# Splitting 20 of the 24 weights of k, r and v during the first FFN, with a round trip through DRAM

## The chip, the cores and the metric

The kernel runs on one core of a Trainium2 chip. TensorE (PE) does the matmuls, VectorE (DVE) and ScalarE (ACT) the elementwise work, GpSimd (POOL) small preparations and some transfers; SyncE (SP) only issues transfers. The metric is the device time of one execution in microseconds, the median of several runs.

## The reference

A trunk of two layers over 512 tokens of width 1024, in fp32: a gated linear recurrence (RG-LRU), a gated conv-FFN, an RWKV-7 time mixing, a second conv-FFN, and a norm. The change concerns the FFN and the first products of RWKV-7:

```
def _conv_ffn(x, norm, w_up, conv_w, conv_b, w_down):
    h = _rmsnorm(x, norm)
    u = jnp.einsum('btd,df->btf', h, w_up)
    gate = _causal_dwconv(u[..., :D_FF], conv_w, conv_b)
    hid = jax.nn.gelu(gate, approximate=True) * u[..., D_FF:]
    return jnp.einsum('btf,fd->btd', hid, w_down)

def _rwkv7_block(...):
    xs_rkv = jnp.stack([h + xx * mix[0], h + xx * mix[1], h + xx * mix[2]])
    rkv = jnp.einsum('sbtd,sde->sbte', xs_rkv, w_rkv)
    ...
    y = _rwkv7_scan(rh, hs(decay), kh, vh, -kk, kk * ah)
    ...
    return jnp.einsum('btd,de->bte', y * g, w_out)
```

## The kernel before

**Products.** A product of fp32 matrices is made of three matmuls of rounded parts (mm3, matmuls at L54): a weight's high part with the activation's high and low part, and its low part with the high part. So every weight must be split: ACT casts the raw piece to its high part (wh, L94) and DVE subtracts that from the raw piece (wl, L97). A piece is 512 KB, 128 partitions x 1024 numbers, and so are wh and wl.

**Weights.** plan_weights (L100) lists all pieces in the order of use. Numbers 33 to 100 are the first FFN's, 101 to 108 those of k, 109 to 116 of r, 117 to 124 of v, 125 to 132 of RWKV's output, and then the second FFN's. weights_load (L160) issues the raw piece's load on SP's queue (L166); a few FFN pieces have a second part that POOL adds to them in a transfer (L168). weights_split (L172) does the two splitting instructions. Each product calls next_weights, which loads up to three pieces ahead and splits two ahead. raw, wh and wl (and hi, lo of the FFN's Halves pairs) all live in one ring of 21 slots, b4: a load waits until the last reader of its slot's former content is done, which is a DVE subtraction for a raw piece and a matmul for a split one.

**Stages by time of the profile.** RG-LRU until about 163 us; the first FFN until 548; RWKV-7 until 893 (k until about 613, r until 687, v until 745, then the chunks of the scan and the output); the second FFN to the end. In the FFN, 12 pairs of column blocks are made; every second pair from the third on (Halves, L676 to L785) shares products to save matmuls, and after each of those follows down(n), the product with w_down, which runs between the products of the next pair. Such a round takes 63.75 us. In down, a call between runs the next pair's products up to its third, and a call then makes the weights of what follows.

**Order.** The order of instructions on each engine is the program's, made when the kernel is built: tasks in lanes are pushed (L59) and advanced by background (L62), a few steps after each product. In RWKV the lanes hold the preparation of k and r for the scan, and solve (L1258), a chain of DVE and PE steps for each half of the heads: solve(0) while r is made, solve(1) while v is made. In RWKV the engine POOL makes selectors (sel, selk), masks (L1367), the start of the solve's X (L1297) and copies (tu, rts).

Of the kernel before, what the change touches and what calls it, by code (L numbers as in the profile page):

```python
# [7 lines left out]
F32 = mybir.dt.float32  # L8
F32R = mybir.dt.float32r
# [4 lines left out]
DRAM = bass.MemoryType.DRAM  # L14
NOSYNC = mybir.DependencyInfo(mybir.DependencyClass.NoSync, mybir.DependencyReason.DATA)

P = 128
D = 1024
# [10 lines left out]
WARM2 = 20  # L29
WARM = 14  # L30

HALVES = (3, 5, 7, 9, 11)
# [12 lines left out]
class Kernel:  # L45
# [54 lines left out]
    def plan_weights(self):  # L100
# [45 lines left out]
        full(I["lru_w_out"][0], [0, 1])  # L146
        ffn(0)
        for i in (1, 0):
            full(I["rwkv_w_rkv"][0, i], [0, 1])
# [7 lines left out]
        self.plan = plan  # L157
        self.loaded, self.splitted = {}, {}
        self.n_load = self.n_split = self.n_used = 0

    def weights_load(self, upto):
        while self.n_load < min(upto, len(self.plan)):
            i = self.n_load
            src, k, _, more = self.plan[i]
            raw = self.b4(F32, (k, D // k), f"raw{i}")
            self.nc.sync.dma_start(raw, src)  # L166
            if more is not None:
                self.nc.gpsimd.dma_start(raw, more, accum_op=ALU.add)  # L168
            self.loaded[i] = raw
            self.n_load += 1  # L170

    def weights_split(self, upto, pin=False):  # L172
        while self.n_split < min(upto, len(self.plan)):
            i = self.n_split
            if self.plan[i][2]:
                self.n_split += 1
                continue
            self.weights_load(i + 1)
            raw = self.loaded.pop(i)
            k = self.plan[i][1]  # L180
            hi = self.b4(F32R, (k, D // k), f"wh{i}")
            lo = self.b4(F32R, (k, D // k), f"wl{i}")
            for j in range(k) if i == 0 else [slice(0, k)]:
                self.split(raw[:, j], hi[:, j], lo[:, j], pin=pin)
            self.splitted[i] = (hi, lo)
            self.n_split += 1
# [46 lines left out]
    def setup(self):  # L233
# [4 lines left out]
        self.xsp = ctx.enter_context(tc.tile_pool(name="xsp", bufs=1))  # L238
        dram = ctx.enter_context(tc.tile_pool(name="dram", bufs=1, space=DRAM))
        self.xd = dram.tile([P, KB, T], F32, name="xd")  # L240
# [345 lines left out]
    def ffn(self, l, xs, finish, after=None):  # L586
        nc, tc = self.nc, self.tc
        last = l == 1
        with tc.tile_pool(name=f"ffn{l}", bufs=1) as pool:
# [3 lines left out]
            rbs, norm = [], []  # L593
            gpads = [pool.tile([P, 2, T + 2], F32, name=f"gpad{i}") for i in range(2)]
            for u in gpads:
# [80 lines left out]
            class Pair:  # L676

                def __init__(pair, n):
                    pair.n, pair.gp = n, gpads[n % 2]
                    pair.w, pair.bank, pair.s = {}, {}, {}  # L680

                def gate(pair, e):
                    if not e:
                        pair.ge = pool.tile([P, 2, T], F32, tag="ge", name="ge", bufs=2)
                    fb = 2 * pair.n + e
# [11 lines left out]
            class Whole(Pair):  # L697
# [5 lines left out]
                def product(pair, p):  # L703
                    hi, lo = self.next_weights()
                    k0 = int(p[1]) * 4
                    for e in range(2):
# [9 lines left out]
                        if p == "U1":  # L716
# [6 lines left out]
                            self.split(un, pair.hid[:, e, 0], pair.hid[:, e, 1])  # L723
                        self.background(1)

            class Halves(Pair):
# [95 lines left out]
            def down(n, b0, blocks, between, then):  # L822
# [3 lines left out]
                for g in range(2):  # L826
# [28 lines left out]
                    else:  # L855
# [12 lines left out]

                        self.project(hids, ev, kb=blocks, join=2 if g else 1, rate=0.5 if final else 2, after=hook, x0=b0)

            rooms = []

            def room(b):
                if b % 2 == 0:
                    rooms.append(pool.tile([P, 2, 2, T], F32R, tag="xt", name="hx", bufs=4))
                return rooms[-1][:, b % 2, 0], rooms[-1][:, b % 2, 1]

            for n in range(3, 12, 2):
                products((n, 7))
                if n == 11 and not last:  # L880
                    self.norm_begin()
                    self.push(self.lora_weights())
                down(n, 2 * n - 6, 4 if n < 11 else 8, lambda: products((n, 3)), lambda: ahead(at[0] + 2))
            if not last:
# [896 lines left out]
```

## Time and profile before

| what | us |
|---|---|
| runs | 1292.97, 1290.55, 1290.84 |
| median | 1290.84 |
| the profiled execution | 1291.05 |
| its span, first to last instruction | 1289.3 |

The profile is of one execution. Its page has the busy time of each engine, the span in 40 slices, and groups of instructions by line; the trace behind it answers questions for a window, a tile or an engine. A row of a window gives its length, the busy time of each engine with the number of instructions, PE's granted clock (1.00 is full speed), the mean busy share of the core's 16 DMA engines and the GB/s that they moved. In a row of the timeline stand start and duration, engine, line, operation, out<-in and, in brackets, the idle time ahead of it and what ended it. A DMA's time to landing runs from its issue until its data are there.

### The profile page before, as it was taken

To read this page: it belongs to the slowest core of one execution; us is meant where nothing else is said; L and a number is where in the kernel's file an instruction comes from. 1 tells how busy PE (TensorE), PEld (TensorE's weight loads), DVE (VectorE), ACT (ScalarE), POOL (GpSimd) and SP (SyncE) were. 2 spreads that over 40 slices of the span, in tenths; PEclk is the share of its full clock that TensorE was granted. 3 is DMA by queue.
4 is the path that set the end of the run, shared out by engine and by line. 5 is a ranking of instruction groups with operands and counts; after the bars stand their busy time and mean duration, and the time that the engine had idled before them with its cause. 6 is when DMAs were issued, how large, how long until landed. Compare 5 with 4: busy or idle time off the path is not lost. (4 is left out here: it accounts for less than half of the span.)

```text
span 1289.3 us, 22401 instructions
## 1 busy us (share of the span) xinstructions
PE 1264.2 (98%) x9259; PEld 1067.0 (83%) x9259; DVE 928.1 (72%) x1412; ACT 642.8 (50%) x1006; POOL 133.6 (10%) x206
## 2 busy tenths in 40 slices
PE   9999999999999999999899999999999999999998
PEld 8777888989898888877678888778889898988886
DVE  5998678757575766788999967778766566666653
ACT  6797455434343443559844346545644334343432
POOL 3000001010101010010002145410010101010100
PEclk9999999999999999999999999999999999999999
DMA  7312335455454544422212122132344454545431
GB/s 222 111 55 94 98 122 108 150 112 159 103 164 98 170 95 116 144 79 82 79 41 87 52 62 84 44 99 82 116 96 161 101 170 92 178 84 179 100 131 65
DMA packets 117829, 141.37 MB, mean 110 GB/s; under 512 B 10138, under 2 KB 91748, under 8 KB 117600
## 3 DMA queue, kind: packets, MB, share of 16 engines
q1 hardware_dynamic: 100528, 122.44, 29.8%
q0 software_dynamic: 16624, 16.47, 8.4%
q8 instruction: 72, 1.18, 0.4%
q10 hardware_dynamic: 576, 1.05, 0.2%
q14 instruction: 29, 0.24, 0.1%
HBM read 135.41 MB, written 4.52 MB: 109 GB/s over the span
## 5 line engine op out<-in xcount | busy, mean ns | idle before, releaser
L97 DVE TENSOR_TENSOR wl<-raw,wh 128x1024 fp32r<-128x1024 f32 (+1 forms) x161 | 194.4, 1213 | 124.7 <-ACT wh L94 104.0
L94 ACT CAST wh<-raw 128x1024 fp32r<-128x1024 f32 (+1 forms) x161 | 165.9, 1043 | 195.2 <-PE acc L54 56.0
L54 PE MATMUL accG<-xs,wh 128*128 128x512 f32 x448 | 138.7, 391 | 0.0
L54 PE MATMUL accU<-xs,wh 128*128 128x512 f32 x448 | 138.6, 391 | 0.0
L54 PE MATMUL acc<-hid,wh 128*128 128x512 f32 x384 | 119.8, 395 | 0.0
L744 DVE TENSOR_TENSOR lo<-raw,hi 128x1024 fp32r<-128x1024 f32 x70 | 85.5, 1222 | 39.4 <-PE accU L54 32.0
L743 ACT CAST hi<-raw 128x1024 fp32r<-128x1024 f32 x70 | 73.6, 1052 | 60.7 <-PE accU L54 25.3
L54 PEld LDWEIGHTS accG<-xs,wh 128*128 128x128 f32 x448 | 83.7, 188 | 17.3
L54 PEld LDWEIGHTS accU<-xs,wh 128*128 128x128 f32 x448 | 83.7, 188 | 17.2
L54 PE MATMUL accG<-xs,wl 128*128 128x512 f32 x224 | 87.3, 390 | 0.0
L54 PE MATMUL accU<-xs,wl 128*128 128x512 f32 x224 | 87.3, 390 | 0.0
L54 PEld LDWEIGHTS acc<-hid,wh 128*128 128x128 f32 x384 | 71.3, 187 | 16.7
L54 PE MATMUL accA<-xt,hi 128*128 128x256 f32 x480 | 83.4, 277 | 0.0
L54 PE MATMUL acc<-xs,wh 128*128 128x512 f32 x256 | 81.1, 398 | 0.0
L690 DVE SCALAR_TENSOR_TENSOR cv<-gpad,pv,cv 128x512 f32<-128x512 f32 x96 | 69.1, 748 | 12.3 <-ACT cv L688 11.8
L845 PE MATMUL acc<-wl,hid 128*128 128x512 f32 (+1 forms) x200 | 77.2, 386 | 0.0
L844 PE MATMUL acc<-wh,hid 128*128 128x512 f32 (+1 forms) x200 | 77.0, 385 | 0.0
L843 PE MATMUL acc<-wh,hid 128*128 128x512 f32 (+1 forms) x200 | 76.7, 383 | 0.0
L168 POOL DMA_DIRECT2D raw<-in_ffn_w_up_dram x20 | 25.7, 1285 | 480.8 <-DMA raw<-in_ffn_w_up_dram 336.3
L54 PE MATMUL acc<-hid,wl 128*128 128x512 f32 x192 | 75.0, 395 | 0.0
L54 PEld LDWEIGHTS accA<-xt,hi 128*128 128x128 f32 x480 | 73.2, 188 | 0.9
L54 PE MATMUL accA<-xt,lo 128*128 128x256 f32 x240 | 66.3, 276 | 0.0
(411 smaller groups left out, 2943.1 us busy)
## 6 DMA issues: line engine op xcount, KB each, us to landing
raw<-in_ffn_w_up_dram SPq DMA_DIRECT2D x106, 512.0 KB, 3.7
raw<-in_ffn_w_down_dram SPq DMA_DIRECT2D x48, 512.0 KB, 3.9
raw<-in_ffn_w_up_dram POOLq DMA_DIRECT2D x30, 512.0 KB, 5.9
raw<-in_rwkv_w_rkv_dram SPq DMA_DIRECT2D x24, 512.0 KB, 3.7
raw<-in_lru_w_in_dram SPq DMA_DIRECT2D x16, 512.0 KB, 4.3
raw<-in_lru_w_out_dram SPq DMA_DIRECT2D x8, 512.0 KB, 3.7
raw<-in_rwkv_w_out_dram SPq DMA_DIRECT2D x8, 512.0 KB, 3.6
xd<-x SPq DMA_DIRECT2D x8, 256.0 KB, 2.0
```

Source lines behind the costliest of these rows:

```text
L54: mm = lambda *a, **kw: self.nc.tensor.matmul(ps, *a, skip_group_check=more, **kw)
L94: put = (self.nc.vector.tensor_copy if dve else self.nc.scalar.copy)(hi, src)
L97: self.nc.vector.tensor_tensor(lo, src, hi.bitcast(F32), ALU.subtract)
L168: self.nc.gpsimd.dma_start(raw, more, accum_op=ALU.add)
L690: nc.vector.scalar_tensor_tensor(cv, pair.gp[:, e, j : j + T], cw(j), cv, ALU.mult, ALU.add)
L743: nc.scalar.copy(hi, f[p])
L744: tt(lo, f[p], hi.bitcast(F32), ALU.subtract)
L843: nc.tensor.matmul(ps, hh[:, s], wh[:, k, m], start=kk == 0, stop=False)
L844: nc.tensor.matmul(ps, hl[:, s], wh[:, k, m], start=False, stop=False)
L845: nc.tensor.matmul(ps, hh[:, s], wl[:, k, m], start=False, stop=kk == blocks - 1)
```

## The change

A new task, split_ahead, runs in lane 1 from the first FFN's third pair on. For each of the weights 101 to 120 POOL fetches the raw piece into a tile of the FFN's own pool (early, two buffers), ACT and DVE split it into two slots of the ring (eh, el), and POOL stores both parts to DRAM (whd, wld). It advances by 0.19 step per step of down and 0.25 per product of a Whole pair; what is left is drained ahead of the last down. When RWKV comes to such a weight, weights_load has POOL fetch the two parts from DRAM (two transfers of 512 KB) where SP fetched the raw piece before, and weights_split does nothing for it. Room for early is made by one gate pad (gpad) and one ge buffer in the first FFN where there were two. between and then now also split the weights that down needs next, which moves those requests in both FFNs.

```diff
+AHEAD = 20
@@ plan_weights
         ffn(0)
+        self.ahead = range(len(plan), len(plan) + AHEAD)
@@ weights_load
             src, k, _, more = self.plan[i]
+            if i in self.stored:
+                self.loaded[i] = tuple(self.b4(F32R, (k, D // k), f"{part}{i}") for part in ("wh", "wl"))
+                for t, d in zip(self.loaded[i], self.stored[i]):
+                    self.nc.gpsimd.dma_start(t, d)
+                self.n_load += 1
+                continue
             raw = self.b4(F32, (k, D // k), f"raw{i}")
             self.nc.sync.dma_start(raw, src)
...
+    def split_ahead(self, pool):
+
+        raws, parts = {}, {}
+        n = self.ahead.stop
+
+        for i in range(self.ahead.start, n + 2):
+            if i < n:
+                src, k = self.plan[i][:2]
+                raws[i] = pool.tile([P, k, D // k], F32, tag="early", name="early", bufs=2)
+                self.nc.gpsimd.dma_start(raws[i], src)
+            if i - 2 in parts:
+                k = self.plan[i - 2][1]
+                self.stored[i - 2] = [self.dram.tile([P, k, D // k], F32, name=f"{part}d{i - 2}") for part in ("wh", "wl")]
+                for t, d in zip(parts.pop(i - 2), self.stored[i - 2]):
+                    self.nc.gpsimd.dma_start(d, t.bitcast(F32))
+            if i - 1 in raws:
+                k = self.plan[i - 1][1]
+                parts[i - 1] = [self.b4(F32R, (k, D // k), f"{part}{i - 1}") for part in ("eh", "el")]
+                self.split(raws.pop(i - 1), *parts[i - 1])
+            yield 1
@@ weights_split
+            if i in self.stored:
+                self.splitted[i] = raw
+                self.n_split += 1
+                continue
@@ ffn
-            gpads = [pool.tile([P, 2, T + 2], F32, name=f"gpad{i}") for i in range(2)]
+            gpads = [pool.tile([P, 2, T + 2], F32, name=f"gpad{i}") for i in range(1 + l)]
@@ Pair
-                    pair.n, pair.gp = n, gpads[n % 2]
+                    pair.n, pair.gp = n, gpads[n % len(gpads)]
...
-                        pair.ge = pool.tile([P, 2, T], F32, tag="ge", name="ge", bufs=2)
+                        pair.ge = pool.tile([P, 2, T], F32, tag="ge", name="ge", bufs=1 + l)
@@ Whole
                         self.background(1)
+                        self.background(0.25, 1)
@@ down
-                        self.project(hids, ev, kb=blocks, join=2 if g else 1, rate=0.5 if final else 2, after=hook, x0=b0)
+                        self.project(hids, ev, kb=blocks, join=2 if g else 1, rate=0.5 if final else 2, rate1=0 if final else 0.19, after=hook, x0=b0)
@@ the loop over the pairs
+            def between():
+                products((n, 3))
+                if n < 11:
+                    self.weights_split(self.n_used + 2)
+
+            def then():
+
+                if len(seq) > at[0]:
+                    self.weights_split(self.n_used + 2)
+                ahead(at[0] + 2)
+
             for n in range(3, 12, 2):
                 products((n, 7))
+                if n == 3 and not last:
+                    self.push(self.split_ahead(pool), 1)
                 if n == 11 and not last:
+                    while self.tasks[1]:
+                        self.background(1, 1)
                     self.norm_begin()
                     self.push(self.lora_weights())
-                down(n, 2 * n - 6, 4 if n < 11 else 8, lambda: products((n, 3)), lambda: ahead(at[0] + 2))
+                down(n, 2 * n - 6, 4 if n < 11 else 8, between, then)
```

Three places of the order. The first is ACT in the first FFN, in the round whose first down weight is 67. Before, with hi1 to hi7 the casts of the Halves pair, cv and ge its gate, and raw62 to raw66 its pieces:

```order
L743 CAST hi5_3034<-raw63_2951 128x1024
L743 CAST hi6_3074<-raw62_2949 128x1024
L688 ACTIVATE cv_3011<-gpad0_1477,pv_78 128x512
L743 CAST hi2_3106<-raw64_2954 128x1024
L691 ACTIVATE ge_3010<-cv_3011 128x512
L688 ACTIVATE cv_3029<-gpad0_1477,pv_78 128x512
L691 ACTIVATE ge_3010<-cv_3029 128x512
L94 CAST hid_3050<-s_3051 128x512
L743 CAST hi7_3137<-raw65_2956 128x1024
```

And of the change, where the helper's line is L96, Halves' L778 and the gate's L722 and L725:

```order
L96 CAST eh108_3061<-early_2971 128x1024
L778 CAST hi1_3065<-raw62_3015 128x1024
L96 CAST wh61_3069<-raw61_3013 128x1024
L778 CAST hi5_3110<-raw63_3017 128x1024
L96 CAST eh109_3155<-early_3055 128x1024
L722 ACTIVATE cv_3087<-gpad0_1477,pv_78 128x512
L778 CAST hi6_3160<-raw62_3015 128x1024
L722 ACTIVATE cv_3105<-gpad0_1477,pv_78 128x512
L725 ACTIVATE ge_3086<-cv_3087 128x512
L778 CAST hi2_3192<-raw64_3020 128x1024
```

eh108 and eh109 have come in among the casts of the pair, and hi6, hi2 and hi7 now stand behind eh109. In both orders hi4, hi3 and then wh67, the cast of the down weight, follow some rows below.

The second is POOL in the same round. Before it issued only three transfers in a round, each of which adds a second part to a raw piece (raw63, raw65 and raw62 in this one, behind two of the round before):

```order
L168 DMA raw52_2428<-in_ffn_w_up_dram 128x4x256
L748 DMA raw49_2421<-in_ffn_w_up_dram 128x4x256
L168 DMA raw63_2951<-in_ffn_w_up_dram 128x4x256
L168 DMA raw65_2956<-in_ffn_w_up_dram 128x4x256
L748 DMA raw62_2949<-in_ffn_w_up_dram 128x4x256
```

Now the same three stand among stores and fetches:

```order
L177 DMA raw63_3017<-in_ffn_w_up_dram 128x4x256
L195 DMA whd108_3151<-eh108_3061 128x1024
L177 DMA raw65_3022<-in_ffn_w_up_dram 128x4x256
L190 DMA early_3149<-in_rwkv_w_rkv_dram 128x2x512
L195 DMA wld108_3152<-el108_3062 128x1024
L195 DMA whd109_3442<-eh109_3155 128x1024
L190 DMA early_3440<-in_rwkv_w_rkv_dram 128x2x512
L195 DMA wld109_3443<-el109_3156 128x1024
L783 DMA raw62_3015<-in_ffn_w_up_dram 128x4x256
```

So each transfer that adds waits behind what those stores and fetches wait for.

The third is RWKV. ACT before, at the weights 107 and 108 (pinv, fac, sq, ppad and AR belong to the preparation of k and r, mt to the mixing of the input, back to k's norm):

```order
L962 ACTIVATE mt_5389<-x_68,om_451 128x512
L1172 ACTIVATE ppad1_5255<-AR0_4902 128x8x64
L94 CAST wh107_5334<-raw107_5262 128x1024
L1171 ACTIVATE fac_5358<-BK0_4904,oka_452,pv_78 128x512
L1170 ACTIVATE sq_5356<-BK0_4904,pv_78 128x512
L1149 CAST back_5375<-back_5370 40x512
```

ACT now, at the same place:

```order
L1012 ACTIVATE mt_5575<-x_68,om_451 128x512
L1222 ACTIVATE ppad1_5445<-AR0_5100 128x8x64
L1221 ACTIVATE fac_5544<-BK0_5102,oka_452,pv_78 128x512
L1233 COPY AR0_5100<-ppad1_5445 128x4x2x64
L1220 ACTIVATE sq_5542<-BK0_5102,pv_78 128x512
L1199 CAST back_5561<-back_5556 40x512
```

The casts are gone from it. On POOL the fetches stand in their place; at the weights 116 and 117 it now reads:

```order
L171 DMA wl116_6043<-wld116_4130 128x1024
L1417 MEMSET masks_6221 128x384
L1488 COPY rts_6214<-AR0_5100 64x128
L1424 AFFINE_SELECT masks_6221<-masks_6221 64x64 x9
L1488 COPY rts_6214<-AR0_5100 64x128 x3
L171 DMA wh117_6118<-whd117_4213 128x1024
L171 DMA wl117_6119<-wld117_4214 128x1024
```

Before, the masks and copies stood alone there; the loads of the raw pieces were on SP.

More of the change, by code (lines that the diff above doesn't have):

```diff
@@ L157, in plan_weights @@
         self.plan = plan
-        self.loaded, self.splitted = {}, {}
+        self.loaded, self.splitted, self.stored = {}, {}, {}
         self.n_load = self.n_split = self.n_used = 0
@@ L238, in setup @@
         self.xsp = ctx.enter_context(tc.tile_pool(name="xsp", bufs=1))
-        dram = ctx.enter_context(tc.tile_pool(name="dram", bufs=1, space=DRAM))
+        dram = self.dram = ctx.enter_context(tc.tile_pool(name="dram", bufs=1, space=DRAM))
         self.xd = dram.tile([P, KB, T], F32, name="xd")
```

## The prediction

> **What bounds the kernel now.** I read the busy times first, then the slices, then windows by stage, and last the waits of the stage that the change touches.
>
> ```profile
> PE 1264.2 (98%) x9259; PEld 1067.0 (83%) x9259; DVE 928.1 (72%) x1412; ACT 642.8 (50%) x1006; POOL 133.6 (10%) x206
> DVE  5998678757575766788999967778766566666653
> ```
>
> PE is busy 98% of the span; what is left to win is its 2% of idle time and whatever stretches its matmuls. DVE has its row of nines in slices 20 to 23, about 612 to 741 us: the RWKV layer's k, r and v. The windows of that layer and of one 63.75-us round of the first FFN say the same:
>
> ```profile
> 288.75:352.50 63.75, 63.75 (x362) 55.57 (x362) 41.65 (x52) 24.99 (x31) 3.81 (x3) 1.00 0.51 133
> ...
> 613.90:632.00 18.10, 15.04 (x65) 10.88 (x64) 17.05 (x30) 15.19 (x29) 0.00 (x0) 0.91 0.20 65
> 632.00:650.00 18.00, 16.88 (x184) 12.45 (x185) 14.61 (x23) 14.04 (x32) 2.76 (x2) 1.00 0.26 83
> 650.00:677.00 27.00, 25.98 (x119) 19.41 (x118) 26.75 (x59) 11.21 (x17) 1.83 (x6) 1.00 0.15 45
> 677.00:703.40 26.40, 26.40 (x298) 23.32 (x299) 25.79 (x55) 12.33 (x29) 3.39 (x11) 1.00 0.30 96
> 703.40:710.20 6.80, 5.57 (x155) 5.18 (x154) 4.94 (x4) 4.18 (x9) 6.20 (x6) 1.00 0.19 64
> 710.20:744.40 34.20, 30.91 (x606) 27.63 (x604) 32.11 (x78) 13.18 (x25) 3.63 (x9) 1.00 0.14 44
> ```
>
> The columns are length, then busy time of PE, weight loads, DVE, ACT and POOL, then granted clock, DMA share and GB/s. In the FFN, PE is full, DVE has 22.1 us free in a round, ACT 38.8, the DMA engines half. In the six RWKV windows, 130.5 us together, PE is busy 120.78 and DVE 121.25: there DVE is the fuller engine.
>
> Where PE waits there, and for whom:
>
> ```profile
> PE acc L54 <- ACT wh L94: 3.5, 2, 3.0
> PE pe L1462 <- DVE tu L1507: 1.8, 2, 1.1
> PE tr L1432 <- DVE W L1425: 1.5, 1, 1.5
> PE knb L1211 <- DVE rec L1205: 1.2, 1, 1.2
> ```
>
> ```profile
> 615.89 1.03 ACT L94 CAST wh<-raw 128x1024 fp32r<-128x1024 f32 x1
> ...
> 616.97 3.25 PE L54 MATMUL acc<-mix,wh 128*128 128x512 f32 x7 [3.02 <-ACT wh L94]
> ```
>
> ```profile
> 614.00:617.00 3.00, 0.03 (x1) 0.03 (x1) 3.00 (x6) 3.00 (x7) 0.00 (x0) 1.00 0.53 175
> 617.00:621.00 4.00, 4.00 (x11) 3.09 (x11) 4.00 (x7) 4.00 (x9) 0.00 (x0) 0.57 0.03 6
> ```
>
> The longest wait is for the cast of weight 107: ACT, busy all of 614 to 617, comes to it late. PE then runs four microseconds at a granted clock of 0.57.
>
> **The change, part by part.** A split is one cast and one subtraction:
>
> ```profile
> L97 DVE TENSOR_TENSOR wl<-raw,wh 128x1024 fp32r<-128x1024 f32 (+1 forms) x161 | 194.4, 1213 | 124.7 <-ACT wh L94 104.0
> L94 ACT CAST wh<-raw 128x1024 fp32r<-128x1024 f32 (+1 forms) x161 | 165.9, 1043 | 195.2 <-PE acc L54 56.0
> ```
>
> *Taken out of the RWKV layer.* Twenty splits: 20 x 1.21 = 24.3 us of DVE and 20 x 1.04 = 20.9 us of ACT. The subtractions by window:
>
> ```profile
> 613.90:632.00 18.10, 6.51 (x17) 3.15 (x16) 3.65 (x3) 0.91 0.20 65
> 632.00:650.00 18.00, 6.80 (x17) 3.19 (x17) 2.45 (x2) 1.00 0.26 83
> 650.00:677.00 27.00, 13.00 (x34) 6.20 (x33) 4.86 (x4) 1.00 0.15 45
> 677.00:703.40 26.40, 14.48 (x48) 9.09 (x48) 4.88 (x4) 1.00 0.30 96
> 703.40:710.20 6.80, 2.25 (x9) 1.51 (x9) 1.18 (x1) 1.00 0.19 64
> 710.20:744.40 34.20, 11.53 (x41) 7.65 (x41) 2.43 (x2) 1.00 0.14 44
> ```
>
> (The third figure with a count is DVE's on wl.) Between 613.9 and 710.2 the sum is 17.0 us. The two after 710.2 are weights 121 and 122, which are still split there. So:
> - The wait for weight 107 goes, 3.02 us, and with it the low clock, 4 x (1 - 0.57) = 1.7 us. Together 4.7. What is late next there is not a weight (108 comes ready made too) but the key's norm, with 1.2 us of waiting for rec, which DVE feeds.
> - PE's other idle time in the six windows is 9.72 - 3.02 = 6.70 us, and the waits named for it are on DVE results. From below it gives nothing (DVE runs a chain whose links must follow each other); from above all 6.7. The last window keeps its two splits and its 94% of DVE, so I leave its 3.29 us where they are and take the rest, 3.4.
>
> Gain 8.1 us, by these rows between 3 (4.7 less about as much waiting for rec again) and 11.4 (9.72 + 1.7). Matmuls that now run spread out could close up as well; that cannot be more than the 17.0 us that DVE loses.
>
> *Added to the first FFN.* The same 24.3 and 20.9 us, five splits in a round: DVE goes from 41.65 to 47.7 of 63.75 us, ACT from 24.99 to 30.2. Their idle time hides it at no cost; without this cover the price would be the 24.3 us themselves. One gate pad and one ge instead of two cost nothing:
>
> ```profile
> 311.94 2.74 DVE L690 SCALAR_TENSOR_TENSOR cv<-gpad,pv,cv 128x512 f32<-128x512 f32 x4
> ...
> 316.39 1.29 DVE L783 TENSOR_TENSOR s<-s,ge 128x512 f32<-128x512 f32 x2
> ...
> 343.49 0.69 DVE L714 TENSOR_TENSOR gpad<-accG,rb 128x512 f32<-128x512 f32 x1 [0.32 <-PE accG L54]
> ```
>
> The pad's last reader ends at 314.7 and the next pair writes at 343.5; ge is last read until 317.7, and the next pair's is made after that pad. Some 28 us lie between.
>
> *The first down weight of a round* is the tight place, and the order shows that its neighbours move:
>
> ```profile
> 357.14 3.09 SPq L166 DMA_DIRECT2D raw<-in_ffn_w_down_dram  x2
> ...
> 361.91 1.23 DVE L97 TENSOR_TENSOR wl<-raw,wh 128x1024 fp32r<-128x1024 f32 x1 [3.58 <-ACT wh L94]
> ...
> 365.38 0.62 PE L54 MATMUL acc<-hid,wh 128*128 128x512 f32 x2
> ```
>
> Weight 67 is loaded from 357.14 (into the slot that the last piece hi4, lo4 of the pair frees), is split at 363.14 and used at 365.38: 2.24 us to spare, as at 301.68 a round earlier. Now eh109 and el109 stand ahead of that piece on ACT and DVE (1.04 and 1.21 us, part of it in idle time), so I expect some 1.2 us of the margin to go, and 1.0 to remain. Transfers that meet others are slower, by how much the page shows:
>
> ```profile
> raw<-in_ffn_w_up_dram SPq DMA_DIRECT2D x106, 512.0 KB, 3.7
> raw<-in_ffn_w_down_dram SPq DMA_DIRECT2D x48, 512.0 KB, 3.9
> raw<-in_ffn_w_up_dram POOLq DMA_DIRECT2D x30, 512.0 KB, 5.9
> raw<-in_lru_w_in_dram SPq DMA_DIRECT2D x16, 512.0 KB, 4.3
> q1 hardware_dynamic: 100528, 122.44, 29.8%
> q0 software_dynamic: 16624, 16.47, 8.4%
> ```
>
> The first layer's loads, which meet all that the kernel fetches at its start, took 4.3 instead of 3.7: 0.6, within the 1.0. I take 0.5 us for the FFN over all its rounds; from below 0, from above the slower rival's price.
>
> *Transfers.* Five fetches, ten stores of 512 KB in a round are new, all issued by POOL. By the hardware queue's rate (122.44 MB in 29.8% of 1289.3 us: 319 GB/s) one takes 1.64 us of the 16 engines, 15 of them 24.7 us, and the share goes from 0.51 to 0.90. By the software queue's (16.47 MB in 8.4%: 152 GB/s, nearly all transfers that add to what they find) 3.45 us each, share 1.32, more than there is. Plain copies are nearer to the first row. The Trainium skill, "DMA: Bandwidth & Descriptors", Issuing engines are not separate DMA queues, speaks against the change: DMAs of all issuers interleave on the same 16 engines, so POOL's queue keeps nothing out of SP's way. The same page's Anatomy of one DMA — SWDGE (gpsimd) path gives 2.0 us + bytes / 436e3, an estimate of 3.2 us for each of these; the 5.9 us on POOL's queue above disagrees (those add), and by the page the next item's price would be nothing and the sum 0.5 us better.
>
> *Fetches in the RWKV layer* take the place of SP's 20 loads: 40 on POOL, in ring order, each held until its slot is free; selectors, masks, and the solve's X stand behind them in that queue. The one without room is weight 117:
>
> ```profile
> 678.92 1.05 POOL L1438 COPY rts<-AR 64x128 f32<-64x128 f32 x3
> ...
> 687.19 0.28 PE L1250 MATMUL acc<-wh,mix 128*128 128x256 f32 x1
> ```
>
> It stands behind these copies and can go out at about 680.0; with two issues and 5.9 us it lands between 686 and 687.2, and PE wants it at 687.19. Between nothing and some 1.5 us; I take 0.5. Weight 118 is used seven microseconds later and has room.
>
> *The second FFN* keeps its two pads; its down weights are only requested a few rows later. Cost 0.
>
> **The sum**: -4.7 - 3.4 + 0.5 + 0.5 = -7.1 us on the profiled run's own 1291.05 (span 1289.3 and 1.75 around it), 1283.95. The median of the three runs shown is 0.2 lower, 1290.84; I write 1284.
>
> **Rivals.**
> - *Full gain*: DVE is what holds r and v, and without 17 us of splits both solves start sooner. For it: 26.75 of 27.00 and 25.79 of 26.40 us of DVE. Against it: PE is also full in 677 to 703.4. It gives 11.4 us of idle time and clock, and up to 17 with matmuls that close up: 1274 to 1280, near 1278.
> - *Given back*: the wait at 614 moves to rec and to fetches on POOL that are held by their slots; only 0 to 2 us stay, 1289 to 1291. For it: the chain of the second solve fills the last window (32.11 of 34.20) and keeps its splits.
> - *Slower*: the DMA engines become the bound of the FFN. With 49% of 63.75 us free, 31.2 us, fifteen transfers fit if each takes less than 2.08 us of all engines. At 2.4 us, between the two rates, a round misses 4.8 us and four rounds 19; less the 8 gained, 1302. PE would wait for the first down weight of each round. For it: 152 GB/s on that queue. Against it: stores and fetches add nothing to memory.
> - *It does nothing*, because the fetches go out too late: the order has them some weights ahead of their use, except 117, so I give this little.
>
> **How the numbers follow.** Forecast (1280 to 1288) 0.44; full gain 0.16; given back or without effect 0.21; slower 0.19. A measurement tells about 0.2%, 2.6 us, from no change: faster means below 1288.3. Faster gets the first two and a little of the third's lower edge, 0.62; same 0.19; slower 0.19. The range takes in the forecast, the given-back case, most of the full gain and the mild part of the slower one: 1276 to 1297.
>
> **What would show it.** In the changed profile PE's 3.02-us wait near 614 and the low clock behind it are gone; DVE has about 17 us less between 613.9 and 710 and 6 more in each of four FFN rounds; PE stays at 63.75 of 63.75 there; weight 117 is waited for by a microsecond at most. I am wrong if PE waits for wh or wl at the first down weight of a round, if raw pieces on SP take over 4.9 us to land there, or if the stretch from 621 to 744 is as long as before.

## The result, and the profile after

The changed kernel takes 1322.15 us (median of 6 runs, 1321.17 to 1323.92) against 1291.88 of before on the same chip: a ratio of 1.0235, 95% interval 1.0221 to 1.0249. It is 30 us slower, outside the range and on the other side. The profiled run has a span of 1321.5 us, 32.2 more than before. First the page of the changed kernel, busy times, the DMA slices and the queues:

```profile
PE 1281.2 (97%) x9259; PEld 1076.5 (81%) x9259; DVE 929.1 (70%) x1411; ACT 640.1 (48%) x1006; POOL 190.5 (14%) x306
...
DMA  7322444496968678445545120322344546354541
...
q1 hardware_dynamic: 94064, 111.95, 26.6%
q0 software_dynamic: 31024, 68.90, 20.3%
```

DVE and ACT do as much as before. The software queue now has 68.90 MB. If the transfers that it had before still take their 108 us of 16 engines, the 52.43 MB that came on took 20.3% of 1321.5 us less those 108, which is 160 us: an estimate of 328 GB/s, or 1.60 us for 512 KB.

Where the time went is read from the first matmul of one and the same weight in both timelines (before first, then after: weight 101, which opens k, and the first weight of the second FFN):

```profile
572.22 0.62 PE L54 MATMUL acc<-mix,wh 128*128 128x512 f32 x2
...
893.51 0.62 PE L54 MATMUL accG<-xs,wh 128*128 128x512 f32 x2
```

```profile
610.88 0.63 PE L56 MATMUL acc<-mix,wh 128*128 128x512 f32 x2
...
925.10 0.63 PE L56 MATMUL accG<-xs,wh 128*128 128x512 f32 x2
```

At weight 101 the changed kernel is 38.7 us late, at the second FFN 31.6, at the end 32.2. So the stretch up to weight 101, in short the first FFN, lost 38.7 us, RWKV won 7.1, the second FFN cost 0.6. The windows of the changed kernel, the first FFN from where the new task runs, then k, r and v (PE, weight loads, DVE, ACT, POOL, clock, DMA share, GB/s):

```profile
248.00:548.00 300.00, 279.13 (x1485) 237.20 (x1484) 194.20 (x236) 121.30 (x146) 50.82 (x70) 0.97 0.73 217
...
611.00:655.00 44.00, 44.00 (x197) 34.18 (x195) 38.58 (x85) 37.20 (x64) 13.19 (x50) 1.00 0.52 162
655.00:718.00 63.00, 63.00 (x399) 47.86 (x392) 54.74 (x114) 27.38 (x59) 15.58 (x32) 1.00 0.43 140
718.00:776.00 58.00, 56.23 (x1061) 51.39 (x1061) 49.30 (x110) 24.28 (x55) 16.14 (x23) 1.00 0.27 88
```

PE, which had no idle time in the FFN, now misses 20.9 of 300 us there, and the mean clock of 0.97 over the other 279 is some 8 us more. On the whole page PE's busy time grew by 17.0 us (1264.2 before) for the same 9259 matmuls; what stretches them beyond the clock is not shown. In k and r PE is busy all the time. The waits of PE between 225 and 600 us, after:

```profile
PE accU L56 <- ACT wh L96: 11.5, 4, 4.6
PE accA L56 <- ACT s L800: 5.1, 5, 2.6
PE acc L56 <- ACT wh L96: 2.5, 4, 1.0
PE acc L56 <- DVE wl L99: 1.6, 3, 0.5
```

Before, PE waited for no weight of the FFN in this stretch. The largest wait comes once in each of four rounds, at the up weights 48, 61, 74 and 87, one weight ahead of the Halves pair; the first down weight of the round comes after it. One such place, the one with the shortest of the four waits, in the changed kernel's timelines of POOL, ACT and PE:

```profile
275.37 1.32 POOL L177 DMA_DIRECT2D raw<-in_ffn_w_up_dram  x1 [12.32 <-DMA raw<-in_ffn_w_up_dram]
276.16 1.09 POOL L195 DMA_DIRECT2D whd<-eh  x1
```

```profile
282.78 1.04 ACT L96 CAST wh<-raw 128x1024 fp32r<-128x1024 f32 x1 [8.39 <-DMA whd<-eh]
```

```profile
283.88 0.73 PE L56 MATMUL accU<-xs,wh 128*128 128x512 f32 x2 [0.98 <-ACT wh L96]
```

Read backwards: PE waits for wh48; ACT could not cast it, since its ring slot still held an early weight until the store whd had landed; that store went out at 276.16, behind an adding transfer on POOL that had waited 12.32 us for the FFN's own raw piece; and that piece took long to land. In three of the four rounds ACT waits so for a store before it casts this weight, 8.3 to 8.7 us each time. SP's loads wait for the same stores (the longest of SP's waits in the changed kernel, 225 to 560 us):

```profile
SPq L175 <- DMA whd<-eh: 52.2, 4, 13.8
```

And they take longer to land (KB each and median us, between 250 and 540 us; before, then after):

```profile
raw<-in_ffn_w_up_dram SPq DMA_DIRECT2D x32, 512.0 KB, 3.7
```

```profile
raw<-in_ffn_w_up_dram SPq DMA_DIRECT2D x34, 512.0 KB, 9.0
...
wld<-el POOLq DMA_DIRECT2D x20, 512.0 KB, 7.0
```

Three things can thus make the loss: slots of the ring that early weights hold (A), the bytes (B), and the order on the queues, above all POOL's (C). The work of the splits themselves is a fourth (D).

### The profile page after: what moved, and what is told of

It is laid out like the page before. It is cut to its first block, busy times and chain, and to the rows that moved or that the text cites. A ratio compares the mean times of both kernels' runs of the same rounds, so it can differ in the third digit from the quotient of the medians.

```text
span 1321.5 us, 22606 instructions
## 1 busy us (share of the span) xinstructions
PE 1281.2 (97%) x9259; PEld 1076.5 (81%) x9259; DVE 929.1 (70%) x1411; ACT 640.1 (48%) x1006; POOL 190.5 (14%) x306
## 3 DMA queue, kind: packets, MB, share of 16 engines
q0 software_dynamic: 31024, 68.90, 20.3%
## 4 chain that ended last, share of the span: by engine, by line
PE 75%; DVE 9%; DMA 7%; issue 5%; ACT 3%; POOL 1%; SPq 0%; POOLq 0%; DVEq 0%; ACTq 0%
PE acc L56 25%; PE accG L56 9%; PE accU L56 8%; PE accA L56 6%; DMA raw<-in_ffn_w_up_dram 4%; PE acc L880 3%; PE acc L879 3%; PE acc L878 3%; PE accF L56 3%; PE accD L56 1%; DVE wl L99 1%; PE s L1468 1%; DMA whd<-eh 1%; DVE lo L779 1%; PE lg L56 1%
## 5 line engine op out<-in xcount | busy, mean ns | idle before, releaser
L96 ACT CAST wh<-raw 128x1024 fp32r<-128x1024 f32 (+1 forms) x141 | 145.2, 1041 | 178.2 <-DMA raw<-in_ffn_w_down_dram 40.0
L99 DVE TENSOR_TENSOR wl<-raw,wh 128x1024 fp32r<-128x1024 f32 (+1 forms) x141 | 170.0, 1212 | 79.2 <-ACT wh L96 70.6
L56 PE MATMUL accU<-xs,wh 128*128 128x512 f32 x448 | 144.4, 404 | 11.5 <-ACT wh L96 11.5
L56 PEld LDWEIGHTS accU<-xs,wh 128*128 128x128 f32 x448 | 86.7, 195 | 31.0 <-ACT wh L96 13.2
L56 PEld LDWEIGHTS accG<-xs,wh 128*128 128x128 f32 x448 | 83.7, 188 | 17.3
L778 ACT CAST hi<-raw 128x1024 fp32r<-128x1024 f32 x70 | 73.3, 1049 | 42.9 <-PE accU L56 16.1
L56 PE MATMUL accA<-xt,hi 128*128 128x256 f32 x480 | 86.8, 282 | 5.1 <-ACT s L800 5.1
L56 PE MATMUL accU<-xs,wl 128*128 128x512 f32 x224 | 90.3, 403 | 1.1 <-DVE wl L99 1.1
L722 ACT ACTIVATE cv<-gpad,pv 128x512 f32<-128x512 f32 x48 | 38.0, 811 | 66.2 <-DVE gpad L809 40.4
```

The source lines that it names most:

```text
L56: mm = lambda *a, **kw: self.nc.tensor.matmul(ps, *a, skip_group_check=more, **kw)
L96: put = (self.nc.vector.tensor_copy if dve else self.nc.scalar.copy)(hi, src)
L99: self.nc.vector.tensor_tensor(lo, src, hi.bitcast(F32), ALU.subtract)
L722: nc.scalar.activation(cv, pair.gp[:, e, 0:T], AF.Identity, bias=self.vec(f"ffn_conv_b{l}", fb), scale=cw(0))
L778: nc.scalar.copy(hi, f[p])
```

## The experiments

Each time stands beside runs of the kernel before on the same chip; where the FFN alone is tested, RWKV loads and splits its weights as before, so nothing is won there.

### The traffic alone, without splits

```diff
-                parts[i - 1] = [self.b4(F32R, (k, D // k), f"{part}{i - 1}") for part in ("eh", "el")]
-                self.split(raws.pop(i - 1), *parts[i - 1])
+                parts[i - 1] = [raws.pop(i - 1)] * 2
```

> Left out: the splits of split_ahead; each of the 20 raw pieces is fetched in the first FFN and stored twice as it is, nothing of it is read later, and RWKV loads and splits its weights as before. No slot of the ring is held. Theory A (each early weight holds two of the 21 ring slots from before its cast until its stores have landed, so the FFN's own loads and casts come late): the FFN costs 0 to 4 us, 1290 to 1296. Theory B (the transfers fill the 16 DMA engines): most of the FFN's 39 us stays, 1318 to 1331. Theory C (order on POOL's queue: stores and the FFN's adding transfers wait behind each other): a part stays, 1296 to 1312.

Measured: 1331.43 us, ratio 1.0287 (1.0258 to 1.0317). It reads like B, but does not show it. Without splits to pace them the fetches and stores stood in a row on POOL, each waiting for the one before, and the FFN's adding transfers came behind:

```profile
303.31 0.53 POOL L195 DMA_DIRECT2D whd<-early  x1 [4.32 <-DMA early<-in_rwkv_w_rkv_dram]
303.83 0.53 POOL L195 DMA_DIRECT2D wld<-early  x1
305.29 2.65 POOL L177 DMA_DIRECT2D raw<-in_ffn_w_up_dram  x2 [0.93 <-issue]
```

The first of these additions went out at 260.67 in the kernel before. The run says that stores and fetches without any split can cost as much as the change. It has all of their bytes and POOL's order at once, and so does not tell B from C.

### The splits without the stores

```diff
-                for t, d in zip(parts.pop(i - 2), self.stored[i - 2]):
-                    self.nc.gpsimd.dma_start(d, t.bitcast(F32))
+                parts.pop(i - 2)
```

> The stores are left out; the 20 splits are made into ring slots and dropped, and RWKV loads and splits its weights as before. A slot is free as soon as el is written. Theory A: the slots are held some 8 us shorter for each weight, so a part of the 39 us stays, 1297 to 1315. Theory B: a third of the traffic is left, 1291 to 1297. Theory C: without stores POOL's queue has only the fetches, 1290 to 1295. Theory D (the work of ACT and DVE itself makes the FFN late): all stays, 1322 to 1331.

Measured: 1295.40 us, ratio 1.0022 (1.0009 to 1.0034), so 3 us. D falls: the work of ACT and DVE, the fetches, the single gate pad and the moved requests cost 3 us together (weight 101 comes 4.5 us late in its trace, at 576.7). The rest of the loss hangs on the stores.

### The stores on ACT's queue

```diff
-                    self.nc.gpsimd.dma_start(d, t.bitcast(F32))
+                    self.nc.scalar.dma_start(d, t.bitcast(F32))
```

> The 40 stores are issued on ACT's queue in place of POOL's, everything else as in the changed kernel. Theory A and C: a store no longer waits behind the FFN's adding transfers, slots come free sooner, 1290 to 1312 (C: nearly all 39 us go, 1284 to 1292; A: 10 to 25 us go, as slots are still held from before the cast). Theory B: 1320 to 1324, since the bytes are the same.

Measured: 1327.63 us, ratio 1.0258 (1.0200 to 1.0316). Neither A nor C got what it expected, and it is above B's range too. The stores were off POOL, but a store of el now stands on ACT and waits there for DVE, and the casts of the FFN behind it wait too. In ACT's waits of this run between 225 and 590 us:

```profile
ACT hi L778 <- DMA raw<-in_ffn_w_up_dram: 43.1, 9, 6.5
...
ACT eh L96 <- DVE el L99: 23.1, 3, 8.1
ACT eh L96 <- DMA whd<-eh: 12.2, 2, 7.0
```

### A ring with 20 slots

```diff
-N4 = 21
+N4 = 20
```

> The kernel before with 20 slots in the ring in place of 21, nothing else changed. Theory A: slots are scarce, so one less for the whole program costs something, 1295 to 1310, with waits for wh at the same places of the first FFN as in the changed kernel. Theories B, C and D: a slot more or less is no matter, 1290 to 1293.

Measured: 1299.90 us, ratio 1.0053 (1.0034 to 1.0072), some 7 us, though its runs spread from 1295 to 1303. A slot less for the whole program costs something, but not where A said. In the profiled execution (1295.01, the fastest) weight 101 starts at 572.3, as before, and PE waits for no up weight in the FFN; the second FFN starts at 897.0 in place of 893.5, so what this execution lost it lost in RWKV. The early weights take two slots and for a part of the time only (eh ahead of wh48 from its cast at 271.10 until its store had landed at 282.78), so the run neither shows nor excludes that they cost by holding them.

### Raw pieces stored, slots or no slots, POOL or ACT

The first of these stores the raw piece in place of eh and el, from POOL, so that no store holds a slot. Its stores also stand ahead of the next fetch on POOL, where the change has them behind it:

```diff
+                for d in kept:
+                    self.nc.gpsimd.dma_start(d, parts[i - 2])
...
-                for t, d in zip(parts.pop(i - 2), self.stored[i - 2]):
-                    self.nc.gpsimd.dma_start(d, t.bitcast(F32))
```

> As the changed kernel in the FFN, but the two stores of a weight read the raw piece (early) in place of eh and el, so that no store holds a slot of the ring; RWKV loads and splits its weights as before. Against the run without stores (1295) it has the 40 stores more. Theory A (slots held until the stores have landed): 1292 to 1301. Theory B (the transfers fill the 16 DMA engines, or slow the others): 1315 to 1333. Theory C (order on POOL's queue): between, 1300 to 1333, and then the FFN's adding transfers are seen to go out late while the DMA engines have room.

Measured: 1322.20 us, ratio 1.0228 (1.0184 to 1.0272), 29 us, without a slot held by a store. PE's waits are now at accA, for ACT, 18.9 us in four rounds; on POOL the adding transfers stood behind stores that waited 87.2 us for fetches. A is not needed for a large loss; B and C are both in this run.

The second holds the slots to the place of the store, and stores nothing:

```diff
+                for t in parts.pop(i - 2):
+                    seen = pool.tile([P, 1], F32, tag="seen", name="seen", bufs=2)
+                    self.nc.gpsimd.tensor_copy(seen, t[:, 0, 0:1].bitcast(F32))
```

> As the run without stores, but a POOL copy of one column reads eh and el where the changed kernel has the store, so that the slots are held to that point (not for the landing) with no byte stored; RWKV loads and splits as before. Theory A: the slots are held for most of the time that they are in the changed kernel, 1303 to 1325. Theory B: 1293 to 1298, as without stores. Theory C (stores waited for their turn in POOL's order): 1300 to 1325 as well; if so, store_raw tells A and C apart.

Measured: 1311.02 us, ratio 1.0141 (1.0101 to 1.0182), 18 us with no byte stored. PE's idle time is again at accA, once in each of four rounds:

```profile
PE accA L56 <- ACT s L799: 11.1, 4, 4.7
```

The third is the same with the copies on ACT:

```diff
-                    self.nc.gpsimd.tensor_copy(seen, t[:, 0, 0:1].bitcast(F32))
+                    self.nc.scalar.copy(seen, t[:, 0, 0:1].bitcast(F32))
```

> The run that holds the slots up to the stores' place without storing (1311), but ACT makes the two one-column copies in place of POOL, so POOL's queue has only the fetches and the adding transfers, as in the run without stores; RWKV loads and splits as before. Theory A (slots held): 1308 to 1315, the same as with POOL. Theory C (the adding transfers wait on POOL behind instructions that wait for ACT's and DVE's splits): 1294 to 1300. Theory B says 1294 to 1298 as well, and is told from C by the run of raw stores on ACT.

Measured: 1294.21 us, ratio 1.0024 (1.0010 to 1.0037), 3 us, no more than without any holding. These two runs differ in one thing in the program, the engine that makes the copy. POOL and ACT in the run with copies on POOL, at wh48:

```profile
272.19 1.31 POOL L177 DMA_DIRECT2D raw<-in_ffn_w_up_dram  x1 [8.61 <-PE accG L56]
272.96 1.54 POOL L194 COPY seen<-eh 128x1 f32<-128x1 f32 x1
...
287.08 1.31 POOL L782 DMA_DIRECT2D raw<-in_ffn_w_up_dram  x1 [1.56 <-DVE lo L778]
```

```profile
274.53 1.05 ACT L96 CAST wh<-raw 128x1024 fp32r<-128x1024 f32 x1 [1.31 <-POOL seen L194]
...
284.37 1.05 ACT L777 CAST hi<-raw 128x1024 fp32r<-128x1024 f32 x1 [1.72 <-POOL seen L194]
```

And ACT and POOL in the run with copies on ACT:

```profile
267.99 0.19 ACT L194 COPY seen<-eh 128x1 f32<-128x1 f32 x1
...
273.09 0.18 ACT L194 COPY seen<-el 128x1 f32<-128x1 f32 x1
273.18 1.04 ACT L96 CAST wh<-raw 128x1024 fp32r<-128x1024 f32 x1
```

```profile
284.24 1.31 POOL L782 DMA_DIRECT2D raw<-in_ffn_w_up_dram  x1 [1.75 <-DVE lo L778]
```

On POOL the copy of eh comes at 272.96, behind the adding transfer; on ACT at 267.99, right behind its cast and before DVE has made el from it (270.05), so there it holds the slot no longer than no copy would. With the copies on POOL the casts of wh48 and of a hi wait for them (1.31 and 1.72 us), and the third adding transfer of the round goes out 2.8 us later. So 15 us (18 less 3) come with no byte stored when what frees the slots waits its turn on POOL. That is C, and this trace has A as a way in which it reaches PE. That the slots are harmless if held as long by another engine is not shown, since the copies on ACT do not hold them as long.

The fourth stores the raw piece from ACT, right behind the split:

```diff
+                for part in ("wh", "wl"):
+                    self.nc.scalar.dma_start(self.dram.tile([P, k, D // k], F32, name=f"{part}d{i - 1}"), raw)
```

> The run without stores (1295) with 40 stores that wait for nothing: right behind the cast of a weight ACT's queue stores the raw piece twice, so no store holds a ring slot and none stands on POOL's queue; RWKV loads and splits as before. Theory B (the bytes themselves, 21 MB more written in the first FFN): 1312 to 1325. Theories A and C: 1294 to 1301.

Measured: 1334.75 us, ratio 1.0335 (1.0290 to 1.0380). It reads like B and is not clean either: a store of a raw piece needs no cast, so the order put it ahead of eh, and ACT waited in it for the fetch:

```profile
ACT wh L96 <- DMA early<-in_rwkv_w_rkv_dram: 34.4, 3, 11.9
```

The clean run stores eh twice, since that cannot go ahead of its own cast:

```diff
+                for part in ("wh", "wl"):
+                    self.nc.scalar.dma_start(self.dram.tile([P, k, D // k], F32, name=f"{part}d{i - 1}"), hi.bitcast(F32))
```

> The run without stores (1295) with 40 stores that wait only for the cast ahead of them on their own engine: right behind the cast of eh ACT's queue stores eh twice (in place of eh and el); nothing stands on POOL's queue and nothing waits for a fetch or for DVE; RWKV loads and splits as before. The slot of eh is held until both have landed, which the run with copies on ACT (1294) showed to be cheap. Theory B (21 MB more written in the first FFN slow its loads): 1310 to 1325. Theory C (instructions of the FFN stand behind waiting stores in the same queue): 1294 to 1300.

Measured: 1314.14 us, ratio 1.0172 (1.0139 to 1.0205), 22 us, and 19 more than with copies on ACT. These are the bytes that the change moves in the FFN, with no store waiting for anything but its own engine. It is cleaner than the run before but not clean: a store holds the slot of eh until it has landed, and ACT, which waits 1.0 us for fetches in the run with copies on ACT, here waits for them ahead of the cast of eh:

```profile
ACT eh L96 <- DMA early<-in_rwkv_w_rkv_dram: 42.3, 6, 8.0
```

The windows of this run, and its transfers between 262 and 270 us:

```profile
250.00:265.00 15.00, 15.00 (x66) 12.05 (x65) 12.26 (x18) 6.38 (x8) 1.48 (x2) 1.00 0.59 197
265.00:280.00 15.00, 15.00 (x67) 12.39 (x66) 4.43 (x5) 4.21 (x4) 2.27 (x3) 1.00 1.05 327
...
310.00:325.00 15.00, 15.00 (x82) 12.87 (x81) 11.60 (x17) 8.74 (x11) 0.51 (x1) 1.00 0.41 147
...
340.00:355.00 15.00, 15.00 (x72) 12.60 (x71) 7.88 (x9) 6.88 (x8) 3.35 (x3) 1.00 1.12 315
```

```profile
raw<-in_ffn_w_up_dram SPq DMA_DIRECT2D x5, 512.0 KB, 10.8
early<-in_rwkv_w_rkv_dram POOLq DMA_DIRECT2D x1, 512.0 KB, 8.4
whd<-eh ACTq DMA_DIRECT2D x1, 512.0 KB, 6.4
```

A DMA share of 0.70 on the mean is 0.41 in one stretch and full in another, and there the FFN's own loads take 10.8 us, where the kernel before took 3.9. But most of that is not the stores. The run with copies on ACT, which stores nothing and costs 3 us, has in the same stretches:

```profile
265.00:280.00 15.00, 15.00 (x67) 12.35 (x67) 7.64 (x7) 6.58 (x9) 3.32 (x3) 1.00 1.02 259
```

```profile
raw<-in_ffn_w_up_dram SPq DMA_DIRECT2D x4, 512.0 KB, 8.9
```

So 15 us of full engines do not cost PE anything by themselves. Between 250 and 540 us SP's up pieces land in 6.4 us without stores and in 6.3 with them; what the stores lengthen there are POOL's adding transfers, 5.9 to 7.2 us, and the fetches, 6.6 to 7.8. The 19 us belong to the stores, then, and none of them to POOL's order of stores; how much is the bytes (B) and how much the held slots and ACT's waits for fetches is not separated. The Trainium skill, "DMA: Bandwidth & Descriptors", Issuing engines are not separate DMA queues, says that DMAs of all issuers interleave on the same 16 engines; the trace agrees: between 262 and 270 us POOL's queue took 46.0% of the 16 engines, SP's 36.5% and ACT's 14.3%, nearly all of them together.

### Versions that were meant to be faster

In place (eh in a tile of its own, el over the raw piece, no ring slot), stores right behind the split, and stores from ACT with el in place:

```diff
-                parts[i - 1] = [self.b4(F32R, (k, D // k), f"{part}{i - 1}") for part in ("eh", "el")]
-                self.split(raws.pop(i - 1), *parts[i - 1])
+                hi = pool.tile([P, k, D // k], F32R, tag="eh", name="eh", bufs=1)
+                self.nc.scalar.copy(hi, raw.bitcast(F32))
+                self.nc.vector.tensor_tensor(raw, raw.bitcast(F32), hi.bitcast(F32), ALU.subtract)
```

> A version that may beat both: eh in a tile of its own, el written over the raw piece, one buffer of each, so the early weights hold no slot of the ring; fetch, stores, RWKV as in the changed kernel, with twice the steps. Theory A: the FFN costs 0 to 5 us and RWKV's 7.5 us stay won, 1283 to 1290. Theory B: 1318 to 1326. Theory C: each fetch now waits on POOL until the stores ahead have landed, with the adding transfers behind it, 1300 to 1326.

Measured: 1334.73 us, ratio 1.0325 (1.0277 to 1.0372). No slot is held, and it is slower than the change: one buffer makes each fetch wait on POOL for a store's landing, 56.3 us in all, with the adding transfers behind.

```diff
+                self.split(raws.pop(i - 1), *parts)
+                for t, d in zip(parts, self.stored[i - 1]):
+                    self.nc.gpsimd.dma_start(d, t.bitcast(F32))
```

> The changed kernel with each weight's stores written right behind its split in place of one step (some 12 us) later, all else the same. Theory A: slots are held some 10 us less each, half or more of the 39 us go, 1292 to 1308. Theory B: 1318 to 1325. Theory C: the stores are in POOL's order ahead of the adding transfers rather than behind them, 1290 to 1318.

Measured: 1338.54 us, ratio 1.0354 (1.0301 to 1.0407). It is above all three ranges. The stores stand sooner in the order, and the loss is larger, against A: POOL sits 193.6 us in all before stores, waiting for the cast of eh (171.1 in the change), and the adding transfers stand behind.

```diff
+                self.nc.scalar.dma_start(whd, hi.bitcast(F32))
+                self.nc.vector.tensor_tensor(raw, raw.bitcast(F32), hi.bitcast(F32), ALU.subtract)
+                yield 1
+                self.nc.scalar.dma_start(wld, raw.bitcast(F32))
```

> A version that may beat both: eh is stored by ACT's queue right behind its cast, el is written over the raw piece (no ring slot) and stored by ACT's queue half a step later; only the fetches stay on POOL; RWKV fetches ready parts as in the changed kernel. If A and C hold: the FFN costs 3 to 10 us and RWKV's 7.5 us stay, 1285 to 1296. Theory B: 1308 to 1325.

Measured: 1313.57 us, ratio 1.0171 (1.0140 to 1.0202), the best of the versions with all 20 weights ready made, some 8 us ahead of the change, and inside B's range. Weight 101 starts at 601.7 in its trace, so its FFN still loses some 29 us.

### Fewer weights

```diff
-AHEAD = 20
+AHEAD = 8
-rate1=0 if final else 0.19
+rate1=0 if final else 0.08
-                        self.background(0.25, 1)
+                        self.background(0.1, 1)
```

> The changed kernel with 8 weights (k's) in place of 20, the steps spread over the same rounds (rates 0.08 and 0.10). RWKV's gain up to weight 108 was 9.4 us in the changed kernel, and 1.6 of it was given back until 124, so 6 to 9 us stay. Theory C: stores and fetches per round are 40%, and so is the chance that an adding transfer stands behind one: FFN 39 x 0.4 = 16 us, 1297 to 1301. Theory B (the loss comes only where the DMA engines are nearly full, and 40% of the traffic leaves them room): FFN 0 to 5, 1283 to 1290.

Measured: 1299.63 us, ratio 1.0057 (1.0039 to 1.0075), as C expected and well above B's range. In its trace weight 101 starts at 589.5, 17.3 us late, near C's 16: with 40% of the traffic some 45% of the loss is there.

With the weights 105 to 108 alone (rates 0.05 and 0.06):

> The changed kernel with 4 weights (105 to 108) in place of 20, one in a round. Theory C: 39 x 4/20 = 8 us in the FFN, less the 4 to 7 us won at weight 107 and behind: 1291 to 1296. Theory B: the FFN costs nothing, 1284 to 1288.

Measured: 1292.96 us, ratio 1.0006 (0.9993 to 1.0019). The same weights' first matmuls show that its FFN loses 7.9 us until weight 101 and that 5.7 of these are back at weight 109.

With weight 107 alone (rates 0.04 and 0.05):

> The changed kernel with weight 107 alone split ahead (one fetch and two stores in the whole first FFN). By the runs with 4 and 8 weights the FFN costs about 2 us for each, or nothing if only full DMA engines cost; the wait at weight 107 and the low clock behind it, 4.7 us, go; 1 to 2 us are given back at the key's norm and later. If the loss goes with the number of weights: 1288 to 1290. If it needs bursts: 1286 to 1288. If the given-back part eats it: 1290 to 1292.

Measured: 1295.32 us, ratio 1.0023 (1.0010 to 1.0037). Its runs are more spread (1292 to 1300) than those of before beside it (1290 to 1296), and it is no better than four weights. The wait at 107 is gone from its trace, and one wait of 2.0 us at accA in the FFN and a clock of 0.96 between 626 and 760 us have come in; what makes it slower than 1290 stays open. In its trace weight 101 starts at 578.3, 6.1 us late with a single weight ahead, so part of the loss seems not to go with the number of weights; the edits that stay in this run (one gate pad, one ge buffer, the moved requests) were not tested alone.

### The late cast alone

Last, the kernel before with nothing sent through DRAM: the split of weight 107 is asked for one weight earlier.

```diff
-        self.weights_split(i + ahead)
+        self.weights_split(i + ahead + (105 <= i < 106))
```

> The kernel before, with the split of weight 107 asked for one weight earlier (in next_weights of weight 105), which moves its cast 27 rows up in ACT's order; no transfer is added, nothing goes through DRAM. If the gain in k comes from that wait and not from relieving ACT and DVE: 1286 to 1289, as much as 4 or 20 ready weights gained there (5 to 7 us, less what is given back). If the relief is what counts: 1290 to 1292, with the wait moved to weight 108 or to what ACT now does later.

Measured: 1289.59 us against 1293.16, ratio 0.9978 (0.9966 to 0.9989). It is faster than both kernels by a small but clear amount. PE between 610 and 622 us, where the 3.02 us stood, has only

```profile
618.92 1.07 PE L1179 MATMUL ssq<-sq,sel 128*32 128x512 f32 x8 [0.45 <-ACT sq L1170]
621.24 0.66 PE L1194 MATMUL sst<-ident,tmp 128*128 128x128 f32 x4 [0.59 <-ACT tmp L1190]
```

so the wait itself needs an earlier request, and no transfer. It won about 3 us (0.22%).

## Why the prediction was wrong

*The wait at weight 107 and the low clock*, -4.7 us: right as a mechanism. In the changed kernel nothing waits there, and the run with the earlier request wins about 3 us in all without the change.

*The relief of DVE in r and v*, -3.4: right as a sum. Both terms and the cost at 117 (+0.5) made -7.6 for RWKV, and 7.1 were measured. By the first matmuls of the weights k won 5.9 (until 109: 634.26 before, 667.03 after), r and v 4.0 more (until 124: 769.49, 798.25), and 2.7 were given back in the scan's chunks (125: 824.17, 855.67), which I had not priced. That the sum comes so near is in part luck: k, r and v together gave 9.9 where I priced 8.1, and the scan took 2.7 back. The norm's wait for rec did not take the place of the one removed. Weight 117 waits for nothing, so that +0.5 was 0.

*The splits in the first FFN's idle time*, 0: nearly right; without stores they and all the small edits cost 3 us. I priced the single gate pad, the single ge buffer and the moved requests at nothing too; they are in these 3 us.

*The transfers of the first FFN*, +0.5 where 38.7 came: this is the step that failed, and all but 3 to 5 us of it goes with the stores. It failed in two places.
- "0.6, within the 1.0": I took the landing time of the opening (4.3) for that of the crowded FFN, and a share of 0.90 as room. The landing of up pieces became 9.0 us; of that, 6.4 come without any store, at a cost of 3 us, so my sign of 4.9 us was the wrong one to watch. The price per transfer was right, even a little high (1.64 us forecast, 1.60 estimated from the changed kernel), and the mean share stayed at 0.73; but requests come in bursts, and in those the share is at 1. My slower rival asked when the engines are full on the mean of a round (2.08 us each); the loss came without that. The run that stores eh behind its own cast, off POOL's queue, puts 19 us on the stores: the bytes, the slots that they hold until they have landed and ACT's waits for late fetches together.
- POOL's queue was shown in the order and then not priced. I asked for the margin of the first down weight only. A store behind an adding transfer frees its ring slots only after the FFN's raw piece has landed; an adding transfer behind a store or a fetch waits for ACT's and DVE's splits. The pair of runs with copies on POOL and on ACT puts 15 us on it.

3 + 15 + 19 are 37 of the 38.7 us, but that is not a proof. That the three add up in the changed kernel is not shown, since late loads and late stores feed each other there; each was measured in a kernel of its own, and held slots are in the 15 and in the 19.

*The place*: I looked at the first down weight, with 2.24 us to spare. PE does wait for down weights, 2.5 us for wh and 1.6 for wl, which alone is over my 0.5. But the largest wait, 11.5 us, came earlier in the round, at weights 48, 61, 74 and 87, which I did not price at all. In the trace of before weight 48 has 8.6 us to spare (split at 273.71, used at 282.31).

## What to carry to other kernels

Work moved into another stage's idle engines also moves its transfers and its waits: look at the stage in stretches of some 15 us and not at its mean, and go through each queue that they are put on for what stands behind. Full DMA engines alone are not the sign: here 15 us of them cost nothing without stores, and the loss came where instructions stood behind a late transfer. An instruction that frees a buffer is better put where nothing ahead of it waits for a transfer; one-column copies cost 15 us more on POOL than on ACT here. And look first whether the wait that is to go can be had by asking earlier: one line won here what 100 transfers could not.

## What was not expected of the hardware

Loads of 512 KB on SP took 10.8 us in a stretch of 8 us in which 16 engines were busy by 97% at 303 GB/s (stores from ACT), 8.9 in the same stretch at 326 GB/s without stores (copies on ACT), and 3.9 for the one load in that stretch of the kernel before. Copies between SBUF and DRAM on the software queue ran at 328 GB/s by the estimate above, as fast as the hardware queue's 319; the 152 GB/s of that queue in the kernel before belonged nearly all to transfers that add. And the round trip's fetches landed in 4.7 us, the raw pieces on the same queue in 6.3:

```profile
early<-in_rwkv_w_rkv_dram POOLq DMA_DIRECT2D x20, 512.0 KB, 6.3
...
wh<-whd POOLq DMA_DIRECT2D x20, 512.0 KB, 4.7
```
